# Small tiles moved to a pool of their own, so that the operands of products lie multiples of 256 bytes apart in SBUF

## The chip, the cores and the metric

The kernel runs on one core of a Trainium2 chip. The metric is device time in microseconds of one execution. Times come from runs of the whole kernel; the profile is of one execution.

## The reference

A trunk of four pre-norm residual layers over 256 tokens of width 1024, all float32. The mixer of a layer is latent attention (layers 0 and 3), a Conformer convolution module (1) or a gated linear recurrence, HGRN2 (2); each layer then has a SwiGLU block and a gated embedding. Cut to its frame:

```
for i in range(4):
    u = rmsnorm(h, norm1_g[i])
    h = h + (mla, conv, hgrn2)[i % 3](u)
    u = rmsnorm(h, norm2_g[i])
    gate, up = split(u @ w_gu[i], 2)            # 1024 x 5632
    h = h + (silu(gate) * up) @ w_down[i]       # 2816 x 1024
    h = h + (p[i] @ ple_w_proj[i]) * sigmoid(rmsnorm(h, ple_norm_g[i]) @ ple_w_gate[i])
return rmsnorm(h, final_norm_g)
```

## The kernel before, in words

The 256 tokens are two row tiles, h0 and h1, of 128 x 1024, which stay in SBUF. Weights stream in from HBM in granules of 128 x 1024 numbers (tile `raw`). A product of two float32 matrices is made of three products in a one-pass float32 type: a number is split into a high part, rounded, and the rest. ScalarE writes the high part of a weight granule (`whi`, line 189 or, with the norm's gain folded in, 194), VectorE the rest (`wlo`, lines 190 and 195). Activations are transposed on TensorE against an identity (`split_T`, line 259) and split in the same way into pairs of tiles: `xT` for the normed residual and the mixers' outputs, `aT` for the SwiGLU activations, `cT` for the latents of the attention, `pT` for the layer embeddings.

All these products are issued on line 216, three in a row by `mm` (lines 221 to 226): high by high, high by rest, rest by high. Each has a streamed operand and a loaded operand of 128 x 128. In most of them the weights stream, 512 columns at a time, and a 128 x 128 piece of `xT`, `aT`, `cT` or `pT` is loaded before each product; in the first projections of the convolution and part of those of the recurrence the weights are loaded and 256 columns of `xT` stream. In the profile a loaded operand is a LDWEIGHTS on PEld and a product a MATMUL on PE. Names of the form out<-in give the streamed operand first: mm<-whi,xT streams whi against a loaded piece of xT and writes a PSUM bank called mm.

SwiGLU (`ffn`, line 354) runs over 11 blocks of 256 hidden channels. For each block and row tile, `up` makes 24 products into an mm bank with `xT` loaded, and `down` makes 12 into acc banks with `aT` loaded. The gate (`gate`, line 447) makes products into acc banks with `xT` loaded.

A scheduler and slot allocator lays out the instructions and the tiles. Pools follow each other in SBUF: `const`, `wpool` (whi, wlo, raw), `act`, and behind them a pool for each block that is opened and closed. In a pool each tag has its slots behind each other, in the order in which the tags first appear; a slot is rounded up to 32 bytes a partition. The act pool holds the two tiles h, and then, mixed, large tiles and the tiny tiles of the norms: sums of squares (`ss`, `sst`, lines 79 and 85) and the steps of the reciprocal square root (`rs_m`, `rs_y`, `rs_h`, `rs_t`, lines 268 to 286; `rhalf`, line 452). These have one to four numbers a partition. The first of them, `rs_m`, has four slots of 32 bytes right behind h1, ahead of `xT`.

Of the kernel before, what the change touches and what calls it, by code (L numbers as in the profile page):

```python
# [12 lines left out]
F32 = mybir.dt.float32  # L13
# [8 lines left out]
P = 128  # L22
# [29 lines left out]
GAINS = {}  # L52
for _k in GSIZE:
    GAINS[_k] = sum(GSIZE[j] * GCOUNT[j] for j in GAINS)


class Norm:
# [3 lines left out]
    def __init__(self, T, full=False, defer=False):  # L61
        self.T, self.full, self.defer = T, full, defer
        self.x, self.r = None, [None] * NT
# [64 lines left out]
class Trunk:  # L128
    def __init__(self, ctx, tc, a, out):
        self.ctx, self.tc, self.nc, self.a, self.out = ctx, tc, tc.nc, a, out  # L130
        nc = self.nc
        pool = lambda name, **k: ctx.enter_context(tc.tile_pool(name=name, **k))
        self.const = pool("const", bufs=1)
        self.wpool = pool("wpool", bufs=1)
        self.act = pool("act", bufs=1)
        self.ps = pool("ps", bufs=1, space=PSUM)
        self.n = 0
        self.fence = []
        self.head = None
        self.pinned = False  # L140
        self.pT, self.pph = {}, {}
        self.ident = self.const.tile([P, P], F32, name="ident")
        make_identity(nc, self.ident)
        self.gT = self.const.tile([P, a["gains"].shape[1]], F32, name="gT")
        self.h = [self.act.tile([P, D], F32, name=f"h{t}", tag=f"h{t}") for t in range(NT)]

    def nm(self, s):
# [8 lines left out]
        return self.bank("acc", 4)  # L156

    def tmp(self, tag, shape, bufs, dtype=F32, pool=None):
        return (pool or self.act).tile(shape, dtype, name=self.nm(tag), tag=tag, bufs=bufs)

    def scope(self, name):
        return self.tc.tile_pool(name=name, bufs=1)
# [404 lines left out]
    def mla(self, i, norm, done, pre):  # L567
# [8 lines left out]
        with self.scope(self.nm("mla")) as pool:  # L576
# [5 lines left out]
            for t in range(NT):  # L582
                xs, r = self.cut(norm.x, t), norm.r[t]
                pa, pb = self.acc(), self.acc()
                self.mms(pa[:, :QL], xs, [(hi[:, 0, :QL], lo[:, 0, :QL]) for hi, lo in gr])
                self.mms(pb[:, : KVL + ROPE], xs, [(hi[:, 0, QL : NC + ROPE], lo[:, 0, QL : NC + ROPE]) for hi, lo in gr])
                cg = tmp("cg", [P, NC], 1)
                nc.scalar.activation(cg[:, :QL], pa[:, :QL], AF.Copy)
                V.tensor_copy(cg[:, QL:], pb[:, :KVL])
                ss = tmp("css", [P, 2], 2)  # L590
                for c, (ps, n) in enumerate([(pa, QL), (pb, KVL)]):
                    nc.scalar.activation(self.tmp("junk", [P, 512], 1, BF16)[:, :n], ps[:, :n], AF.Square, scale=r, accum_out=ss[:, c : c + 1])
                kr = tmp("kr", [P, 1, ROPE], 2)
                nc.scalar.activation(kr[:, 0], pb[:, KVL : KVL + ROPE], AF.Copy, scale=r)
                self.split_T(cg, cT, 0, t)
                css.append(ss)
                krot.append(kr)
# [579 lines left out]
```

## Time and profile before

| | us |
|---|---|
| median of 3 runs | 1401.75 (1401.49 to 1403.82) |
| profiled execution | 1402.8 |
| its span, first to last instruction | 1401.0 |
| TensorE busy | 1352.4 |
| VectorE busy | 919.4 |
| ScalarE busy | 789.7 |

The granted TensorE clock was 0.992 of full speed over the span. The core read 222.27 MB from HBM, 159 GB/s over the span.

How to read it: the page gives the busy time of each engine and the chain of work that ended last, followed back from the last instruction. Since products are pipelined and their ends are modelled, the mean duration of one (some 400 ns for 512 columns) overlaps that of the next. The chain of waits cuts the time into pieces that don't overlap: a piece "4.18 PE mm L216 x18" is 18 products of line 216 in 4.18 us. In a timeline, the step from one row's start to the next is the pace.

### The profile page before, as it was taken

To read this page: it belongs to the slowest core of one execution; us is meant where nothing else is said; L and a number is where in the kernel's file an instruction comes from. 1 tells how busy PE (TensorE), PEld (TensorE's weight loads), DVE (VectorE), ACT (ScalarE), POOL (GpSimd) and SP (SyncE) were. 2 spreads that over 40 slices of the span, in tenths; PEclk is the share of its full clock that TensorE was granted. 3 is DMA by queue.
4 is the path that set the end of the run, shared out by engine and by line. 5 is a ranking of instruction groups with operands and counts; after the bars stand their busy time and mean duration, and the time that the engine had idled before them with its cause. 6 is when DMAs were issued, how large, how long until landed. Compare 5 with 4: busy or idle time off the path is not lost.

```text
span 1401.0 us, 20409 instructions
## 1 busy us (share of the span) xinstructions
PE 1352.4 (97%) x7153; PEld 1096.6 (78%) x7153; DVE 919.4 (66%) x1995; ACT 789.7 (56%) x1494; POOL 19.1 (1%) x52
## 2 busy tenths in 40 slices
PE   7899999999898999999999999999999999999997
PEld 6767878887875788887788887878878767888885
DVE  6867555558876855556887768555567776655556
ACT  6776555546525654555675546555556776555543
POOL 0100000000000000000000000000000000000000
PEclk9999999999998999999999999999999999999999
DMA  7524656536564655554474425555553433665532
GB/s 234 176 67 128 201 175 191 188 123 220 182 181 153 196 181 180 181 180 163 122 211 132 133 91 175 185 181 181 180 169 110 139 121 108 217 189 187 188 119 74
DMA packets 174023, 228.15 MB, mean 163 GB/s; under 512 B 11712, under 2 KB 138848, under 8 KB 173920
## 3 DMA queue, kind: packets, MB, share of 16 engines
q1 hardware_dynamic: 173920, 226.85, 51.6%
q8 instruction: 56, 0.92, 0.3%
q14 instruction: 47, 0.39, 0.1%
HBM read 222.27 MB, written 1.05 MB: 159 GB/s over the span
## 4 chain that ended last, share of the span: by engine, by line
PE 77%; DVE 8%; DMA 6%; ACT 6%; issue 2%; SPq 0%; DVEq 0%; ACTq 0%
PE mm L216 42%; PE acc L216 26%; PE tr L259 3%; DVE wlo L195 3%; ACT whi L194 2%; DMA raw<-in_ple_w_gate_dram 1%; PE acc L1020 1%; DMA raw<-in_conv_w_pw_dram 1%; DMA raw<-in_mla_w_in_dram 1%; DMA raw<-in_ffn_w_down_dram 1%; PE acc L659 1%; ACT p L669 1%; PE tr L641 1%; DVE wlo L190 1%; ACT whi L189 1%
## 5 line engine op out<-in xcount | busy, mean ns | idle before, releaser
L216 PE MATMUL mm<-whi,xT 128*128 128x512 f32 x1632 | 553.4, 402 | 1.0 <-ACT xT L246 0.7
L194 ACT ACTIVATE whi<-raw,gT 128x512 fp32r<-128x512 f32 (+3 forms) x604 | 387.7, 700 | 136.4 <-PE acc L216 60.1
L195 DVE SCALAR_TENSOR_TENSOR wlo<-raw,gT,whi 128x512 fp32r<-128x512 f32 (+3 forms) x604 | 410.4, 729 | 60.3 <-PE acc L216 33.9
L216 PEld LDWEIGHTS mm<-whi,xT 128*128 128x128 f32 x1632 | 306.3, 189 | 67.1 <-ACT xT L246 1.2
L216 PE MATMUL mm<-wlo,xT 128*128 128x512 f32 x816 | 323.7, 397 | 1.1 <-DVE wlo L190 1.1
L216 PE MATMUL acc<-whi,aT 128*128 128x512 f32 x704 | 234.5, 394 | 1.6 <-DVE aT L247 1.6
L190 DVE TENSOR_TENSOR wlo<-raw,whi 128x1024 fp32r<-128x1024 f32 x120 | 146.4, 1223 | 73.1 <-ACT whi L189 72.7
L189 ACT ACTIVATE whi<-raw 128x1024 fp32r<-128x1024 f32 x120 | 126.1, 1059 | 97.7 <-DMA raw<-in_ffn_w_down_dram 65.9
L216 PEld LDWEIGHTS mm<-wlo,xT 128*128 128x128 f32 x816 | 154.3, 189 | 32.1 <-DVE wlo L190 1.4
L216 PE MATMUL acc<-whi,xT 128*128 128x512 f32 (+2 forms) x544 | 168.9, 386 | 2.3 <-ACT xT L246 2.1
L216 PEld LDWEIGHTS acc<-whi,aT 128*128 128x128 f32 x704 | 131.7, 188 | 34.4 <-DVE aT L247 4.0
L216 PE MATMUL acc<-wlo,aT 128*128 128x512 f32 x352 | 137.6, 391 | 0.0
L373 DVE SCALAR_TENSOR_TENSOR ga<-mm,rs_y,sg 128x256 f32<-128x256 f32 x88 | 42.3, 481 | 142.3 <-ACT sg L371 142.3
L371 ACT ACTIVATE sg<-mm,rs_y 128x256 f32<-128x256 f32 x88 | 41.0, 466 | 138.7 <-PE mm L216 138.2
L216 PEld LDWEIGHTS acc<-whi,xT 128*128 128x128 f32 x544 | 100.5, 191 | 20.4 <-ACT xT L246 2.9
L216 PE MATMUL acc<-wlo,xT 128*128 128x512 f32 (+2 forms) x272 | 103.0, 381 | 0.0
L216 PEld LDWEIGHTS acc<-wlo,aT 128*128 128x128 f32 x352 | 66.1, 188 | 14.8
L247 DVE TENSOR_TENSOR aT<-tr,aT 128x256 fp32r<-128x256 f32 x88 | 37.0, 421 | 57.7 <-ACT aT L246 57.7
L216 PEld LDWEIGHTS acc<-wlo,xT 128*128 128x128 f32 x272 | 51.7, 190 | 8.7 <-DVE wlo L195 0.2
L216 PE MATMUL mm<-whi,cT 128*128 128x384 f32 (+1 forms) x160 | 51.1, 377 | 4.9 <-ACT q L629 3.3
L82 ACT ACTIVATE junk<-h 128x512 bf16<-128x512 f32 x48 | 30.0, 625 | 40.1 <-DVE h L348 22.4
L246 ACT ACTIVATE aT<-tr 128x256 fp32r<-128x256 f32 x88 | 32.7, 371 | 29.6 <-PE tr L259 29.6
(252 smaller groups left out, 1459.8 us busy)
## 6 DMA issues: line engine op xcount, KB each, us to landing
raw<-in_ffn_w_gu_dram SPq DMA_DIRECT2D x352, 256.0 KB, 4.3
raw<-in_ffn_w_down_dram SPq DMA_DIRECT2D x88, 512.0 KB, 4.3
raw<-in_ple_w_gate_dram SPq DMA_DIRECT2D x32, 512.0 KB, 4.9
raw<-in_hgrn_w_in_dram SPq DMA_DIRECT2D x64, 256.0 KB, 3.7
raw<-in_mla_w_out_dram SPq DMA_DIRECT2D x16, 512.0 KB, 4.4
raw<-in_conv_w_pw_dram SPq DMA_DIRECT2D x32, 256.0 KB, 4.9
raw<-in_mla_w_in_dram SPq DMA_DIRECT2D x16, 336.0 KB, 4.3
raw<-in_mla_w_uq_dram SPq DMA_DIRECT2D x12, 384.0 KB, 3.7
```

Source lines behind the costliest of these rows:

```text
L82: square = nc.scalar.activation(T.tmp("junk", [P, 512], 1, BF16), h[:, s], AF.Square, accum_out=ss[:, c : c + 1])
L189: self.last_split = nc.scalar.activation(hi[:, :used], raw[:, :used], AF.Copy)
L190: nc.vector.tensor_tensor(out=lo[:, :used], in0=raw[:, :used], in1=hi[:, :used].bitcast(F32), op=ALU.subtract)
L194: self.last_split = nc.scalar.activation(hi[:, s], raw[:, s], AF.Copy, scale=g[k])
L195: nc.vector.scalar_tensor_tensor(out=lo[:, s], in0=raw[:, s], scalar=g[k], in1=hi[:, s].bitcast(F32), op0=ALU.mult, op1=ALU.subtract)
L216: ins = self.nc.tensor.matmul(*args, **kw)
L246: a = self.nc.scalar.activation(hi, src, AF.Copy)
L247: v = self.nc.vector.tensor_tensor(out=lo, in0=src, in1=hi.bitcast(F32), op=ALU.subtract)
L259: nc.tensor.transpose(pt[:, (i - k0) * P : (i - k0 + 1) * P], src[:, i * P : (i + 1) * P], self.ident)
L371: nc.scalar.activation(sg, ps[:, :256], AF.Silu, scale=r)
L373: nc.vector.scalar_tensor_tensor(out=ga, in0=ps[:, 256:], scalar=r, in1=sg, op0=ALU.mult, op1=ALU.mult)
L641: nc.tensor.transpose(pt[:HD, h * P : (h + 1) * P], src[:, h], self.ident)
```

## The change

The tiny tiles get a pool of their own behind the act pool, and one filler tile of 16 numbers a partition (64 bytes) fills that pool up. Their slots are 4 + 4 + 4 + 8 + 4 + 4 + 2 = 30 of 32 bytes, 960 bytes; with the filler 1024. No tile is written or read that was not before, and the filler is never used.

```
+SMALL = ("ss", "sst", "rs_m", "rs_y", "rs_h", "rs_t", "rhalf")
+PAD = 16
@@ Trunk.__init__
         self.act = pool("act", bufs=1)
+        self.small = pool("small", bufs=1)
         self.ps = pool("ps", bufs=1, space=PSUM)
@@
         self.gT = self.const.tile([P, a["gains"].shape[1]], F32, name="gT")
+        self.small.tile([P, PAD], F32, name="pad", tag="pad")
@@ tmp
-        return (pool or self.act).tile(shape, dtype, name=self.nm(tag), tag=tag, bufs=bufs)
+        return (pool or (self.small if tag in SMALL else self.act)).tile(shape, dtype, name=self.nm(tag), tag=tag, bufs=bufs)
```

In the built program, the start of a tile's first slot, in bytes past a multiple of 256 in each partition:

| tile | before | after |
|---|---|---|
| raw, whi, wlo, h | 224 | 224 |
| xT | 96 | 224 |
| pT | 96 | 224 |
| aT, cT (first tiles of the block's pool) | 160 | 224 |
| ident (const) | 128 | 128 |
| kb, q, qf, at, v of the recurrence | 160 | 224 |
| ga (SwiGLU, transposed into aT) | 160 | 224 |

All slots of one of these tags are multiples of 256 bytes long, and the pieces that the products of line 216 take out of xT, aT, cT, pT, whi and wlo start a multiple of 256 bytes into their tile, so the table holds for each of them. The order of the instructions on each engine, the semaphores that they wait for and the transfers are the same in both programs.

## The prediction

> **What bounds the kernel now.** I read the page's summary of engines and of the chain first, then the groups of TensorE instructions with their shapes kept apart, and then the chain stretch by stretch.
>
> ```profile
> PE 1352.4 (97%) x7153; PEld 1096.6 (78%) x7153; DVE 919.4 (66%) x1995; ACT 789.7 (56%) x1494; POOL 19.1 (1%) x52
> PE mm L216 42%; PE acc L216 26%; PE tr L259 3%; DVE wlo L195 3%; ACT whi L194 2%; DMA raw<-in_ple_w_gate_dram 1%; PE acc L1020 1%; DMA raw<-in_conv_w_pw_dram 1%; DMA raw<-in_mla_w_in_dram 1%; DMA raw<-in_ffn_w_down_dram 1%; PE acc L659 1%; ACT p L669 1%; PE tr L641 1%; DVE wlo L190 1%; ACT whi L189 1%
> ```
>
> TensorE is busy for 97% of the span, and the products of line 216 alone are 68% of the chain that ended last (42% into banks called mm, 26% into banks called acc): 0.68 x 1401.0 = 953 us. In the middle of a SwiGLU stage nothing else counts: in this table of one stretch (length, then busy us and instructions of PE, weight loads, DVE, ACT, POOL, then the granted clock, the DMA share and GB/s) TensorE has no idle time at full clock, DVE and ACT are busy for 47.39 and 42.12 of 85 us, and the DMA engines for 0.57.
>
> ```profile
> 555.00:640.00 85.00, 85.00 (x378) 68.92 (x377) 47.39 (x70) 42.12 (x68) 0.00 (x0) 1.00 0.57 184
> ```
>
> So a change that alters the time from one product to the next is worth that time times the products, as far as they lie on the chain.
>
> **What the change does.** Every engine's list of the changed program holds the same instructions in the same order with the same waits, and every transfer has the same size. Only addresses in SBUF differ. So nothing is to be priced but one question: does the time of an instruction depend on where its tiles lie? The groups (count behind the x, then busy us and the mean ns of one) say how many products there are of each kind:
>
> ```profile
> L216 PE MATMUL mm<-whi,xT 128*128 128x512 f32 x1632 | 553.4, 402 | 1.0 <-ACT xT L246 0.7 <-ACT whi L189 0.3
> L216 PE MATMUL mm<-wlo,xT 128*128 128x512 f32 x816 | 323.7, 397 | 1.1 <-DVE wlo L190 1.1
> L216 PE MATMUL acc<-whi,xT 128*128 128x512 f32 x416 | 136.8, 402 | 1.0 <-ACT xT L246 1.0
> L216 PE MATMUL acc<-wlo,xT 128*128 128x512 f32 x208 | 82.4, 396 | 0.0
> L216 PE MATMUL acc<-whi,aT 128*128 128x512 f32 x704 | 234.5, 394 | 1.6 <-DVE aT L247 1.6
> L216 PE MATMUL acc<-wlo,aT 128*128 128x512 f32 x352 | 137.6, 391 | 0.0
> L216 PE MATMUL acc<-xT,whi 128*128 128x256 f32 x256 | 47.7, 288 | 0.6 <-DVE xT L247 0.3 <-ACT xT L246 0.2
> L216 PE MATMUL mm<-xT,whi 128*128 128x256 f32 x256 | 47.6, 284 | 0.0
> L216 PE MATMUL mm<-xT,wlo 128*128 128x256 f32 x128 | 36.8, 287 | 0.0
> L216 PE MATMUL acc<-xT,wlo 128*128 128x256 f32 x128 | 36.6, 286 | 0.0
> ```
>
> The first name behind the arrow streams, the second is the loaded weight. The streamed pieces of whi and wlo start 224 bytes past a multiple of 256. The loaded xT starts at 96 now (distance 128, the farthest that a distance modulo 256 can be), aT at 160 (distance 64). After the change all three are at 224, distance 0. Two other loaded tiles go with these: pT lies like xT, cT like aT. This gives four classes.
>
> X: xT or pT loaded, 512 columns: 1632 + 816 + 416 + 208 = 3072, and pT's 48 + 24 + 16 + 8 = 96 (the counts of its view, below): 3168.
> X': xT loaded, 384 and 288 columns: the page's acc groups count 544 and 272 with all forms, so 544 + 272 - 416 - 208 = 192.
> T: turned round, xT streams and a weight is loaded: 768 of 256 columns, distance 128 now.
> A: aT or cT loaded: 704 + 352 = 1056, and cT's 160 + 80 = 240.
>
> ```profile
> L216 PE MATMUL acc<-whi,xT 128*128 128x512 f32 (+2 forms) x544 | 168.9, 386 | 2.3 <-ACT xT L246 2.1
> L216 PEld LDWEIGHTS acc<-wlo,xT 128*128 128x128 f32 x272 | 51.7, 190 | 8.7 <-DVE wlo L195 0.2
> L216 PE MATMUL mm<-whi,cT 128*128 128x384 f32 (+1 forms) x160 | 51.1, 377 | 4.9 <-ACT q L629 3.3
> ```
>
> ```profile
> L216 PE MATMUL mm<-whi,pT x48: 387/398/796, 28.2 to 821.4; 128*128 128x512 f32 x48
> L216 PE MATMUL acc<-whi,pT x16: 390/392/404, 342.8 to 348.1; 128*128 128x512 f32 x16
> ```
>
> (The first three rows are the page's, the last two the view of tile pT. Of pT and cT the whi rows are shown; each has half as many with wlo.)
>
> **Does distance matter now?** The mean ns above overlap from one product to the next, so I take the chain, whose pieces follow each other without overlap (start, us, what, count). First SwiGLU, where the pieces of 18 load xT and those of 12 load aT; then a long run of gate products (xT) at the end; then a run of class T.
>
> ```profile
> 597.51 4.18 PE mm L216 x18
> 601.70 2.76 PE acc L216 x12
> ...
> 606.07 4.18 PE mm L216 x18
> 610.25 2.76 PE acc L216 x12
> ...
> 614.62 4.19 PE mm L216 x18
> 618.81 2.75 PE acc L216 x12
> ...
> 741.35 5.10 PE mm L216 x43
> ...
> 1375.17 16.11 PE acc L216 x69
> ```
>
> X costs (4.18 + 4.18 + 4.19) / 54 = 232.4 ns, and 16.11 / 69 = 233.5 at the end; A costs (2.76 + 2.76 + 2.75) / 36 = 229.7. T costs 5.10 / 43 = 118.6. The columns, the type and the sequence of loads of X and A are the same, so 2.7 ns a product hang on the loaded tile. Not on the PSUM bank: the 69 go into acc banks as aT's do. Nor on the tile's shape: pT is as small as aT, lies like xT, and runs like xT, 23 products from 342.77 to 348.12, 232.6 each.
>
> ```profile
> 342.77 0.39 PE L216 MATMUL acc<-whi,pT 128*128 128x512 f32 x1
> ...
> 348.12 0.40 PE L216 MATMUL acc<-whi,pT 128*128 128x512 f32 x1
> ```
>
> And there is a place where two reads meet: the next product's weights are loaded from the moment at which a product starts (both at 303.10), so both tiles are read at once.
>
> ```profile
> 303.10 0.39 PE L216 MATMUL acc<-wlo,aT 128*128 128x512 f32 x1
> 303.10 0.42 PEld L216 LDWEIGHTS acc<-whi,aT 128*128 128x128 f32 x2
> ```
>
> What distance 0 costs has no long run. It occurs where the last product of a series is followed by a transpose that loads h (224), or by a turned product that loads whi:
>
> ```profile
> 307.74 0.39 PE L216 MATMUL acc<-whi,aT 128*128 128x512 f32 x1
> 307.98 0.60 PE L259 MATMUL tr<-ident,h 128*128 128x128 f32 x4
> ...
> 700.95 0.40 PE L216 MATMUL mm<-whi,xT 128*128 128x512 f32 x1
> 701.18 0.40 PE L216 MATMUL mm<-xT,whi 128*128 128x256 f32 x2
> ```
>
> The steps are 0.24 and 0.23 us, in a view that rounds to 10 ns. So distance 0 is neither a large stall nor a large gain; 225 and 235 ns bound it on both sides.
>
> **The sum.** I take distance 0 to cost what the best measured distance costs, 229.7 ns: it is the row nearest to 0, and the two steps do not contradict it. X: 3168 x 2.7 = 8.6 us saved; X': 192 x 2.7 = 0.5; A: 0. T has no row at another distance, its bounds are 0 and 768 x 2.7 = 2.1 us, and I take 0, since its two reads change roles. Together 9.1 us. All line-216 products together fill 3168 x 0.2324 + 192 x 0.16 (between 119 and 232 ns by columns) + 768 x 0.1186 + 1056 x 0.2297 + 240 x 0.20 (the same) = 1149 us, of which the chain holds 953, 0.83. Off the chain TensorE is ahead of its weights, and the gain ends in a longer wait. 9.1 x 0.83 = 7.6 us.
>
> The profiled execution took 1402.8 us around its span of 1401.0; with the change 1395.2. The median of the three runs lies 1.05 us lower, so the forecast is 1401.75 - 7.6 = **1394 us**.
>
> Everything else is priced at zero. The thirty slots of small tiles move behind the large ones, but their instructions keep operands and waits. The sums over h, the weight splits on DVE and ACT and the loads keep the addresses of h, raw, whi and wlo; if their durations changed with the outputs' places, the slack in the stretch from 555 to 640 (37.6 us of DVE's 85) would hide it. In the convolution's taps, the recurrence and the attention heads both operands move by the same amount, so their distances stay. The transposes of ga, q, k and og against the identity change theirs by 64 bytes; line 259 is 3% of the chain, 42 us, and a pace altered by 1%, as between X and A, would be 0.4 us either way.
>
> **The rivals.**
>
> 1. Distance counts evenly: if 64 bytes nearer saves 2.7 ns, the next 64 save as much (227.0 ns, inside the bounds). X and X' 3360 x 5.4 = 18.1, A 1296 x 2.7 = 3.5, T 768 x 5.4 = 4.1: 25.7 x 0.83 = 21.3, so 1380.4 us. For it: two points on a line, and T would follow. Against it: the two steps read 0.24 and 0.23, not 0.22 and 0.23.
>
> 2. No effect of distance: 2.7 ns come from something that the change leaves. Then 1401.75 us. For it: only two distances are measured at length, and distance 0 shows no visible gain. Against it: pT beside aT, above. The Trainium skill, "SBUF — State Buffer", section "Who interferes with whom", speaks for this rival: TensorE has two independent read ports, one for the moving operand and one for weight loads, and it and ScalarE never wait on anyone. By that rule no placement changes a product's time, and the kernel stays at 1401.75; the trace's 232.4 against 229.7 does not bear the rule out.
>
> 3. Slower: the place modulo 128 decides. Today xT, whi and wlo all lie at 96 modulo 128, aT and cT at 32; the pairs that agree are the slow ones. After the change all pairs agree, so X stays and A becomes X: 1296 x 2.7 = 3.5 us longer, nearly all on the chain, 1405 us. It decides as soon as X saves less than 1.1 ns a product (3.5 / 3168). For it: the rows fit it as well as they fit my reading, since distance 128 is 0 modulo 128. Against it: nothing in the rows, only that two streams that start level are read by me as the end of the series 128, 64, 0.
>
> 4. Slower by more: streams that start level collide, 235 ns. X and X' lose 3360 x 2.6 = 8.7, A 1296 x 5.3 = 6.9, T 768 x 2.6 = 2.0: 1419 us. The step of 0.24 allows it, the one of 0.23 just.
>
> **How the numbers follow.** Forecast 0.36 (its own range 1390 to 1398: X saves half as much again, or half), rival 1 0.13, rival 2 0.29, rival 3 0.13, rival 4 0.09. A measurement of this kernel can tell about 0.2%, 2.8 us, from no change. Faster: 0.33 of the forecast's 0.36 and rival 1, 0.46. Same: the rest of the forecast, rival 2, and 0.02 of rival 3, 0.34. Slower: 0.11 of rival 3 and rival 4, 0.20. The range leaves out half of rival 1 below and rival 4 above: 1381 to 1407 us.
>
> **What would show it.** In the chain of the changed kernel, pieces of 18 xT products at 4.13 us instead of 4.18, the gate's 69 at 15.9 instead of 16.11, pieces of 12 aT products still at 2.76, and TensorE's busy time near 1344 us. Pieces of 12 at 2.79 with 18 at 4.18 would be rival 3; 4.09 and 2.72 rival 1; no difference anywhere rival 2. The forecast is wrong if distance 0 is not like distance 64, or if another engine moves at all.

## The result

The changed kernel takes 1391.3 us (median of 4 runs, 1389.81 to 1392.6) where the kernel before took 1401.86 (4 runs, 1401.49 to 1403.82). The ratio is 0.9924, 95% interval 0.9909 to 0.9938: 10.6 us faster. The profiled execution has a span of 1389.3 us, 11.7 less than before. TensorE's row of the page (busy us, share of the span, instructions) fell by 12.4 us from 1352.4, its weight loads by 1.8 us, and no other engine's by more than 1.4:

```profile
PE 1340.0 (96%) x7153; PEld 1094.8 (79%) x7153; DVE 918.9 (66%) x1995; ACT 790.2 (57%) x1494; POOL 17.7 (1%) x52
```

The chain of the changed kernel (start, us, what, count; line 216 is now line 223) in the same SwiGLU stage, then a run of class T in the recurrence, then the gate's run at the end:

```profile
559.36 4.12 PE mm L223 x18
563.49 2.72 PE acc L223 x12
...
567.79 4.13 PE mm L223 x18
571.92 2.72 PE acc L223 x12
...
576.23 4.11 PE mm L223 x18
580.34 2.72 PE acc L223 x12
...
736.29 5.15 PE mm L223 x43
...
799.67 7.91 PE mm L223 x66
...
1363.91 15.70 PE acc L223 x69
```

Products that load xT went from 232.4 to (4.12 + 4.13 + 4.11) / 54 = 228.9 ns, the gate's 69 from 233.5 to 227.5. Products that load aT, which the forecast left alone, went from 229.7 to 2.72 / 12 = 226.7. Class T, where xT streams, became slower, 118.6 to 5.15 / 43 = 119.8.

The starts of all products in the trace, to 1 ns, add two things. First, the pace is now regular: after a break it takes about ten products, and then the steps repeat 226, 227, 227 ns. Before, with xT loaded, they ran through 228 to 241 without coming to rest. The gain comes only with this rest. The first two products of a series (products of 512 columns with xT or aT loaded, steps under 250 ns) cost 232.0 and 233.9 ns on average, no less than before (230.4 and 232.6); the tenth to the thirtieth cost 226.6 to 226.9. Over all products without a wait, a loaded xT comes to 228.5 on average instead of 232.6 (512 columns), an aT to 227.0 instead of 229.9.

Second, part of the gain came back as waits (steps more than 12% over the pace). Let each product that loads xT cost the mean step without a wait for its number of columns. These costs fell from 743.9 to 731.0 us in sum, and what the waits add to them grew from 38.1 to 42.1: 12.9 us won, 4.0 given back. The products that load aT won 3.1 and gave back 0.2. How much comes back differs from one execution to the next: in a second trace of the changed kernel (`e12_change_again`, below) the costs are 730.8 us and the waits add 39.6; in three traces of other layouts at distance 0 or 256 they add 37.8 to 39.5. With one trace of the kernel before, the part given back is known only roughly.

One place where a gain goes back in this execution can be read off the chain: the gate of layer 0 and the start of the convolution. Before:

```profile
343.30 5.35 DMA raw<-in_conv_w_pw_dram
...
355.54 29.98 PE acc L216 x239
```

After:

```profile
341.19 6.19 DMA raw<-in_conv_w_pw_dram
...
354.72 30.54 PE acc L223 x239
```

The piece that waits for the convolution's weights starts 2.1 us earlier but ends only 1.3 us earlier (347.38 instead of 348.65). TensorE then idles longer ahead of the transposes of hg, and they run slower (timeline: start, us, and in brackets the idle time before and what ended it). Before:

```profile
353.49 1.07 PE L259 MATMUL tr<-ident,hg 128*128 128x128 f32 x8 [3.65 <-DVE hg L91]
```

After:

```profile
352.22 1.94 PE L266 MATMUL tr<-ident,hg 128*128 128x128 f32 x8 [4.75 <-DVE hg L96]
```

The clock is the reason that the rows offer. In this table (stretch, length, busy us and instructions of PE, weight loads, DVE, ACT, POOL) it stands behind the last (x). The 6 us in which these transposes start had the full clock before and 0.80 after; the next 5 us had 0.66 and 0.56. Before:

```profile
349.00:355.00 6.00, 2.10 (x17) 1.55 (x15) 4.21 (x16) 3.42 (x8) 1.09 (x1) 1.00 0.76 250
355.00:360.00 5.00, 4.66 (x27) 4.47 (x27) 5.00 (x8) 5.00 (x9) 1.27 (x1) 0.66 0.40 127
```

After:

```profile
348.00:354.00 6.00, 1.78 (x9) 1.58 (x9) 4.02 (x16) 2.91 (x7) 1.36 (x1) 0.80 0.56 181
354.00:359.00 5.00, 4.85 (x24) 4.56 (x24) 4.84 (x8) 4.80 (x9) 0.99 (x1) 0.56 0.41 143
```

That the longer idle time brought the clock down is not shown: in the layout with 256 bytes (below) TensorE idled 3.78 us here, close to the 3.65 before, and the same transposes took 1.94 us too. At the end of the 239 products the changed kernel's lead is down to 385.52 - 385.26 = 0.3 us.

### The profile page after: what moved, and what is told of

Read it like the earlier page. It is cut to its first block, busy times and chain, and to the rows that moved or that the text cites. A ratio compares the mean times of both kernels' runs of the same rounds, so it can differ in the third digit from the quotient of the medians.

```text
span 1389.3 us, 20409 instructions
## 1 busy us (share of the span) xinstructions
PE 1340.0 (96%) x7153; PEld 1094.8 (79%) x7153; DVE 918.9 (66%) x1995; ACT 790.2 (57%) x1494; POOL 17.7 (1%) x52
## 4 chain that ended last, share of the span: by engine, by line
PE 79%; DVE 8%; DMA 6%; ACT 5%; issue 2%; SPq 0%; DVEq 0%; ACTq 0%
PE mm L223 43%; PE acc L223 26%; PE tr L266 3%; DVE wlo L202 2%; DMA raw<-in_ple_w_gate_dram 1%; PE acc L1027 1%; ACT whi L201 1%; DMA raw<-in_mla_w_in_dram 1%; DMA raw<-in_conv_w_pw_dram 1%; PE acc L666 1%; ACT p L676 1%; PE tr L648 1%; DVE wlo L197 1%; PE acc L699 1%; DMA raw<-in_mla_w_ukv_dram 1%
## 5 line engine op out<-in xcount | busy, mean ns | idle before, releaser
L223 PE MATMUL acc<-xT,whi 128*128 128x256 f32 x256 | 48.6, 292 | 0.1
```

The source lines that it names most:

```text
L223: ins = self.nc.tensor.matmul(*args, **kw)
```

## The experiments

The theory: what counts is the distance, modulo 256 bytes, between where the loaded tile and the streamed tile start, whatever the tiles are. The rivals: the tile itself (aT is quicker than xT for another reason), the place (a start at some multiple is quick by itself), and a finer question, which product pays. All these kernels hold the instructions, the order and the waits of the changed kernel; only addresses differ. "Ahead" and "behind" say where the loaded tile starts from the streamed one, modulo 256.

### One unused tile behind h1: distances of 128, 64 and 256

```
         self.h = [self.act.tile([P, D], F32, name=f"h{t}", tag=f"h{t}") for t in range(NT)]
+        self.act.tile([P, 32], F32, name="gap", tag="gap")
```

The 32 numbers are 128 bytes; 16 numbers make 64, and 64 make 256.

128 bytes:

> The change with one unused tile of 128 bytes behind h1, so that xT, pT, aT and cT all lie 128 bytes (modulo 256) from whi and wlo, and nothing else between them differs. Distance theory (only the distance modulo 256 between the loaded and the streamed tile counts): products that load xT cost 232.4 ns as before the change, and those that load aT, which never lay there, 232.4 too (18 in 4.18 us, 12 in 2.79 us); time 1404 to 1406 us. Tile theory (aT is quicker than xT for another reason, 2.7 ns before and 1.3 after the change): aT stays 1.3 to 2.7 ns below xT, 12 in 2.76 us; time 1402.

64 bytes behind:

> The same with 64 bytes: the loaded tiles start 64 bytes behind the streamed ones, where aT lay 64 bytes ahead before the change. Distance theory with no sign: xT and aT both at 229.7 ns (18 in 4.13 us, 12 in 2.76 us), time about 1395 us. Distance theory with a sign: both tiles alike, but not at 229.7. Tile theory: xT slower than aT by 1.3 ns or more.

256 bytes:

> The same with 256 bytes. If the distance counts modulo 256 (or a part of it): as the change, 18 products with xT in 4.12 us, 12 with aT in 2.72 us, 1391 us. If it counts modulo 512 or more: xT and aT above 229 ns and a time above 1394 us.

Measured: 1404.47 us at 128 (ratio to the kernel before 1.0027, 1.0003 to 1.0050), 1404.35 at 64 behind (1.0020, 1.0003 to 1.0037), 1391.02 at 256 (0.9928, 0.9899 to 0.9956). Pieces of the chain of SwiGLU with xT (18) and aT (12), at 128:

```profile
581.11 4.20 PE mm L224 x18
585.32 2.80 PE acc L224 x12
```

64 behind:

```profile
588.20 4.20 PE mm L224 x18
592.39 2.80 PE acc L224 x12
```

256:

```profile
582.67 4.13 PE mm L224 x18
586.81 2.72 PE acc L224 x12
```

The tile theory falls: at 128, aT runs at 2.80 / 12 = 233.3 ns like xT, although nothing but its place changed. The distance counts, and modulo 256: 256 is like 0. But it has a sign. Before the change aT lay 64 ahead and ran at 229.7; 64 behind it runs at 233.3. A reading by how far apart the tiles lie, which the forecast and its first rival share, is thereby wrong.

### Everything 32 bytes further up

```
+        self.shift = pool("shift", bufs=1)
         self.wpool = pool("wpool", bufs=1)
...
         self.small.tile([P, PAD], F32, name="pad", tag="pad")
+        self.shift.tile([P, 8], F32, name="shift", tag="shift")
```

> The change with a pool of one unused tile of 32 bytes ahead of the weights' pool: whi, wlo, raw, h, xT, pT, aT, cT all move by 32 bytes and then lie at multiples of 256, their distances unchanged. Distance theory: as the change, 4.12 us for 18, 2.72 us for 12, 1391 us. Place theory (a start at a multiple of 64 or 256 counts by itself, since a read then touches fewer lines): the pace changes, by 0.4 to 2 ns a product, 1383 to 1389 us if it helps.

1387.87 us, 0.9904 of the kernel before (0.9870 to 0.9938), with products as in the change:

```profile
584.49 4.11 PE mm L225 x18
588.60 2.72 PE acc L225 x12
```

A place at multiples of 256 does nothing for the pace of the products. The time lay 3 us below the change's, but on another occasion, so both were run again side by side:

> The change with everything from the weights on moved by 32 bytes, once more, beside the change itself on one chip. If the lower time of its first runs (1387.9 us) was the spread of runs: within 2 us of the change. If the place at multiples of 256 is worth something outside the products: 2 to 4 us below the change.

> The change itself, for comparison on the same chip: 0.992 of the time before, 18 products with xT in 4.12 us, 12 with aT in 2.72 us.

1388.05 us (0.9925, 0.9903 to 0.9947) with the shift and 1387.10 us (0.9909, 0.9887 to 0.9932) for the change itself, beside 1399.04 for the kernel before on that chip. The lower time was the spread of runs and chips; no effect of the place is visible.

### The other distances

32 behind, 32 ahead, 64 ahead and 96 ahead: the same line with 8, 56, 48 and 40 numbers.

> The change with one unused tile of 32 bytes behind h1: the loaded tiles lie 32 bytes behind the streamed ones. If the pace grows evenly from distance 0 to 64 (228.3 to 233.3 ns for xT, 227.0 to 233.3 for aT): xT 230.8 and aT 230.2 ns, 18 in 4.15 us, 12 in 2.76 us, about 1396 us. If only an exact meeting counts (any other distance as bad as 64): 233 for both, 1403 us.

> The same with 224 bytes: the loaded tiles lie 32 bytes ahead of the streamed ones, modulo 256. Even growth from 0 to 64 ahead (229.7 ns): xT 229, aT 228.4 ns, 18 in 4.12 us, 12 in 2.74 us, about 1393 us. If only an exact meeting counts: 229.7 or more for both, 12 in 2.76 us, above 1394 us.

> The change with 192 bytes behind h1: all loaded tiles lie 64 bytes ahead of the streamed ones, modulo 256, where only aT and cT lay before the change. If the distance counts whatever the tile: xT at 229 to 230 ns as aT there (18 in 4.13 to 4.15 us), aT at 229.1 to 229.7 (12 in 2.75 us), 1392 to 1396 us. If xT is quick at distance 0 alone: 18 in 4.19 us, aT at 2.75, 1401 us or more.

> The same with 160 bytes: 96 ahead. Distances of 32 and 64 behind, 32 ahead and 128 all ran at 233 ns; 0 and 64 ahead are quick. If these two are the exceptions: 18 in 4.19 us and 12 in 2.80, 1402 to 1405 us. If quick places lie on one side: below 230 ns, under 1396 us.

32 behind, 1404.38 us in one run (the kernel before 1399.36 on that chip):

```profile
588.62 4.19 PE mm L224 x18
592.82 2.80 PE acc L224 x12
```

32 ahead, 1402.98 us in one run (the kernel before 1399.36 on that chip):

```profile
588.67 4.20 PE mm L224 x18
592.87 2.80 PE acc L224 x12
```

64 ahead, 1388.81 us, ratio 0.9926 (0.9898 to 0.9954):

```profile
583.54 4.13 PE mm L224 x18
587.67 2.75 PE acc L224 x12
...
797.47 7.52 PE mm L224 x66
...
1362.23 15.82 PE acc L224 x69
```

96 ahead, 1405.96 us in one run (the kernel before 1399.04 on that chip):

```profile
582.59 4.20 PE mm L224 x18
586.79 2.80 PE acc L224 x12
```

The expectation of even growth failed at both distances of 32, and so did the thought that quick places lie on one side. Of the seven distances tried, two are quick:

| distance of the loaded tile | xT, ns (18) | aT, ns (12) |
|---|---|---|
| 0, and 256 | 229 | 227 |
| 64 ahead | 229 | 229 |
| 32 ahead, 96 ahead, 128, 64 behind, 32 behind | 233 | 233 |

64 ahead works for xT just as for aT, which no kernel had tried. The distance thus explains both tiles. Class T, where the roles are turned, has its quick place elsewhere. With xT 64 ahead of the weights, the loaded weight lies 64 behind the streaming xT, and 66 products take 7.52 us, 113.9 each, against 7.91 or 119.8 at distance 0. So a turned product is slowest at 0, where the others are quickest (at the other distances tried, 114.9 to 118.8 on average by the starts in the traces), and 64 ahead gives back in the gate (15.82 against 15.70 us) and with aT what it gains there. Its time is not to be told from the change's.

### The change without its filler

```
-        self.small.tile([P, PAD], F32, name="pad", tag="pad")
```

> The change without its filler tile: xT and pT at distance 0 from whi and wlo as in the change, aT and cT 64 bytes ahead as before the change. Distance theory: 18 products with xT in 4.12 us, 12 with aT in 2.76 us; the time is that of the change plus 1056 x 2.7 ns x 0.75 = 2.1 us, 1393 to 1394 us. If the pace of a product with aT hangs on that of the products with xT beside it: 2.72 us for 12, 1391 us.

1390.26 us, ratio 0.9928 (0.9905 to 0.9950); xT at distance 0, aT 64 ahead as before:

```profile
584.39 4.13 PE mm L222 x18
588.52 2.75 PE acc L222 x12
```

Each tile has the pace of its own distance, 4.13 and 2.75 us. The time came some 3 us below the expected 1393 to 1394. What the filler is worth, 1056 products by 2 to 3 ns, is below what the times can tell. Most of the gain of the change is the move of xT.

### Low halves of xT alone at another distance

Here xT's high and low halves get tags of their own; the low ones lie 64 bytes behind whi and wlo. (The heads' qT and kT in the attention take a slot of each.)

```
+        self.gapped = False
...
+        if tag == "xT":
+            hi = self.tmp("xT", [P, nk, S], 2, F32R)
+            if not self.gapped:
+                self.act.tile([P, 16], F32, name="gap", tag="gap")
+            lo = self.tmp("xTl", [P, nk, S], 2, F32R)
+            if not self.gapped:
+                self.act.tile([P, 48], F32, name="gap2", tag="gap2")
+            self.gapped = True
+            return hi, lo
         return tuple(self.tmp(tag, [P, nk, S], bufs, F32R, pool) for _ in range(2))
...
-            qTs, kTs = (self.tmp("xT", [P, 2, HG, S], 4) for _ in range(2))
+            qTs, kTs = (self.tmp(x, [P, 2, HG, S], 2) for x in ("xT", "xTl"))
```

> The change with the low halves of xT alone moved 64 bytes behind whi and wlo; the high halves, aT, pT, cT stay at distance 0. Of three products the second (wlo streams) is the one during which a low half is loaded, and the third (whi streams, marked as not the first of its pair) the one that uses it. Meeting theory (what counts is the tile loaded while a product streams): two products of three at 227 ns and the one that streams wlo at 233. Own-weights theory (what counts is the tile that the product itself uses): the third is the slow one. Together 18 products in 4.12 to 4.16 us either way, aT unchanged at 2.72 us for 12, about 1396 us.

1392.93 us in one run (the kernel before 1399.36 on that chip), 3 us less than expected. The products fall into three groups by name, first of three, third, second (busy us and mean ns of one; these means overlap):

```profile
L224 PE MATMUL mm<-whi,xT 128*128 128x512 f32 x816 | 329.2, 403 | 1.0 <-ACT xT L263 0.7 <-ACT whi L197 0.3
L224 PE MATMUL mm<-whi,xTl 128*128 128x512 f32 x816 | 324.5, 398 | 0.0
L224 PE MATMUL mm<-wlo,xT 128*128 128x512 f32 x816 | 321.7, 394 | 1.1 <-DVE wlo L198 1.1
```

These rows do not decide which product pays, since the ends are modelled. The steps from start to start, averaged over all products without a wait, are 229.4 ns for the first, 229.3 for the second and 233.6 for the third, the one that uses the low half. That is the opposite of what the meeting theory expected (the second slow). In the record, the product that uses the misplaced tile pays, not the one under which it is loaded. If the record's starts lag the reads by a product, the two theories change places, and no run here excludes that. What is shown is that the cost belongs to single products: two of three stay near 229 while one runs at 233.6.

## Why the prediction was right, point by point

The kernel became faster, as forecast, by 10.6 us where 7.6 were expected, and the mechanism, that addresses alone set the pace, held. The rule by which the size was found, that nearer is quicker, did not; that it gave nearly the right pace for xT was luck.

- **That only addresses matter.** Right. Twelve layouts of the same instructions, the kernel before among them, ran from 1387.1 to 1406.0 us, and the times go with the paces of the products.
- **That the 2.7 ns between xT and aT hang on their places, and not on shape or bank.** Right, and now shown by swapping: at 128 both run at 233 ns, 64 ahead both at 229.
- **That distance 0 costs 229.7 ns for xT.** Mis-sized, and for a wrong reason. It measured 228.9 in SwiGLU and 227.5 in the gate. The forecast called the 64 of aT the distance nearest to 0 and took its pace for it; in fact 32 on either side is slow, and 0 is quick by itself. By the prediction's own sign (distance 0 not like distance 64) this step failed: the same aT ran at 229.7 at 64 ahead and at 226.7 at 0. The two steps quoted at distance 0 could not have told it: they round to 10 ns, and a single step is no measure of a series that comes to rest after about ten.
- **A: 0.** Wrong by its size: aT went from 229.7 to 226.7, 1056 x 3.0 = 3.2 us. Rival 1 had this term (2.7 ns), from a line through two points that does not exist.
- **T: 0.** Wrong in sign: +1.2 ns a product, 0.9 us lost. The bounds given, 0 and a gain, left this out.
- **The part on the chain, 0.83.** With the measured paces the sum is 3168 x 3.5 = 11.1 and 3.2, less 0.9: 13.4 us. The span fell by 11.7, 0.87 of it. The 10.6 us of the medians against the forecast's 7.6 is thus the sum's fault (9.1 instead of 13.4), not that of the part on the path. That part is not tested closely: the spans of the five traces with all tiles at distance 0 or 256 lie 11.4 to 15.0 us below the one before.
- **Rival 2** (no effect) fell. The Trainium skill, "SBUF — State Buffer", section "Who interferes with whom", gives TensorE two independent read ports and has it waiting on no one. These runs show the same product at 227 and at 233 ns with nothing changed but addresses, and they decide against the reading that no placement changes a product's time.
- **Rival 3** (modulo 128) fell with the change itself, where xT kept its place modulo 128 and became 3.5 ns quicker. **Rival 4** (level streams collide) fell for the products that load activations; class T shows a small form of it.
- **What would show it.** The pieces of 18 were expected at 4.13 and came at 4.11 to 4.13, those of 12 at 2.76 and came at 2.72, the gate's 69 at 15.9 and came at 15.70; TensorE's busy time, expected near 1344, was 1340.0.

## What to carry to other kernels

Where one-pass float32 products follow each other with a weight load each, the pace depends on where the loaded tile starts relative to the streamed one, modulo 256 bytes: 227 ns against 233 for 512 columns here, which is worth 0.8% of this kernel. Small tiles that a slot allocator drops between large ones set that distance by accident, and so does any later edit that adds one; it is worth printing the addresses, and trying a filler of a few sizes, since the good distances are not a matter of near and far. Before pricing such a gain, look where the products wait for weights: of 16 us won in pace with xT and aT, 4 came back as longer waits in one execution and 2 in another.

## What the runs showed of the hardware that was not expected

The dependence is sharp: 227 to 229 ns at 0 and at 64 ahead, 233 at 32 to either side. With distance 0 the steps settle into 226, 227, 227, and a series has to run for about ten products to get there. The quick distance for 256 columns with a weight loaded is another one (113.9 ns with the loaded tile 64 behind, 119.8 at 0). Why 64 ahead is quick and 32 is not, no run here shows.
